# Scores ahead of their maxima, low key parts above zeros, staged keys and a full-height join in a hybrid attention and experts kernel

## The chip, the cores and the metric

The kernel runs on 1 core of one Trainium2 chip. The metric is device time in microseconds (us), as a median over executions. The engines named below are TensorE (PE, with its weight loads shown apart as PEld), VectorE (DVE), ScalarE (ACT), GpSimd (POOL) and SyncE (SP), which here only issues transfers.

## What is computed

One layer over 512 tokens of width 1024, all in float32. A normalized input is projected to many heads, three attentions follow, gates weigh them, and a routed layer of 16 experts ends it:

```python
n = rmsnorm(h, g_mix[l])
aq, ak, av, iq, ik, iw, bq, bk, bv, mq = split_cols(n @ w_in[l], IN_SPLITS)
y_a = dsa_attention(aq, ak, av, iq, ik, iw)        # top 128 of the keys by an index score, 8 heads
y_b = dilated_attention(bq, bk, bv)                # 3 groups (dilation 1, 4, 16) x 8 heads, joined by their lse
y_m = memory_attention(mq, rmsnorm(mem, g_mem[l]), w_mem_kv[l])   # 4 heads over 256 memory rows
merged = sum_i gates[i] * (y_i @ w_branch[l, i])
h = h + merged @ w_out[l]
h = h + hier_moe(rmsnorm(h, g_ffn[l]), ...)        # 16 experts, two per token
return rmsnorm(h, g_final)
```

In the dilated attention each group gives a softmax output and a log-sum-exp per head; a softmax over the three log-sum-exps joins the groups.

## The kernel before, in words

**Precision.** Every float32 operand is split into a high and a low part, and a product is three matmuls (high·high, high·low, low·high). In the attentions the two parts of a query of 64 values lie above each other: the high part in rows 0 to 63, the low part in rows 64 to 127 (`restack_q`). The keys lie the same way, but with the same part twice: `k2` holds the high part in both halves, `kl` the low part in both halves (`restack_k`, line 532). `scores` (line 255 through the helper `mm`) then takes two matmuls, queries against `k2` and queries against `kl`, with all 128 rows in each.

**Order of the work.** Up to about 505 us the projections run in one stream: for each weight block of 128x1024 a transfer is issued from POOL's queue (L113), ACT writes the high part (L139), DVE or, for blocks 14 to 45, POOL writes the low part (L143, L141), and PE multiplies (tiles `P`). Attention work is cut into segments that are fed into this stream by a count of projection steps (`feed`, `feed_att`, `tick`): `segA` makes scores and softmax, `segB` transposes the probabilities (tiles `T`, L681, L816, L890), `segC` multiplies with the values (tiles `O`). The top-k search of the first attention (`topk_seg`, L611 and L612) runs on DVE in the same way. The framework works out all waits, and puts the instructions of each engine in an order at compile time; each engine then runs its own list in that order, and an instruction that waits holds up those behind it.

**Scores and softmax.** A PSUM tile `S` (two buffers) holds the scores of two blocks of queries, u = 0 and u = 1. For each u in turn `segA` writes the scores and calls `softmax_tile`: DVE adds the mask and takes the maxima into `st` or `dl` (L628), ACT takes the exponential and the row sums (L630). The framework orders a PE write after an earlier DVE read of the same PSUM bank, so the scores of u = 1 wait for the maxima of u = 0.

**Keys and queries of a job.** The dilated attention runs in six jobs (`JOBS`: D0 twice, D12 four times), with the two jobs of the first attention between them. `rope_unit` makes rotated queries or keys in four DVE products and writes high and low parts to two tiles `st` (ACT L504, DVE L505; tag `st`, two buffers, for queries and keys alike). From there SP issues small transfers of 64 KB: 16 for the queries of a job (L522), 32 for the keys (L532). `k2` and `kl` share four buffers of tag `k2`, two tiles each.

**The join.** After the last job, `betas` makes the weights of the groups as `e2` (128 tokens x 32 columns per block), PE transposes them to 32 rows (L760), ACT copies them to `eT` of 32 rows, and `y_pair` spreads them over 128 rows by eight matmuls of 32 rows with a 0/1 matrix `pick` (tiles `T` from `eT`), whose results DVE multiplies into the outputs (L783, L784). They stand among the last gate projections, at 496 to 505 us.

**The rest.** From 505 us come the branch products (`B`), the output projection, routing, and from about 755 us the experts (`A`, `Y`).

Of the kernel before, what the change touches and what calls it, by code (L numbers as in the profile page):

```python
# [237 lines left out]
def hybrid_kernel(ctx, tc, A, out):  # L238
    nc = tc.nc
# [101 lines left out]

    def stat_x(i):
        rsx[i] = cst.tile([128, 4], F32, name="rsm", tag="rsm", bufs=3)
        scr = ap_.tile([128, 1024], F32, name="scr", tag="k2", bufs=4)
        rms(xt(i), scr, rsx[i])

    def norm_x(i):
# [130 lines left out]
    def lhs_nat(t, k):  # L478
        return nTh[:, k, 128 * t:128 * t + 128], nTl[:, k, 128 * t:128 * t + 128]

    def rope_unit(perm, then):

        t = {}

        def first():
            for i, tab in ((1, cosT), (3, sinT)):
                t[i] = rp.tile([128, 512], F32, name="t%d" % i, tag="rt", bufs=4)
                nc.vector.tensor_mul(t[i], PA, tab)

        def second():  # L490
            for i, tab in ((2, sinT), (4, cosT)):
                t[i] = rp.tile([128, 512], F32, name="t%d" % i, tag="rt", bufs=4)
                nc.vector.tensor_mul(t[i], PB, tab)
            res = []
            for (a, b, op) in ((t[1], t[2], OP.subtract), (t[3], t[4], OP.add)):
                st = rp.tile([128, 2, 512], F32R, name="st", tag="st", bufs=2)
                nc.vector.tensor_tensor(a, a, b, op=op)  # L497
                if perm:
                    av = a.rearrange("p (i r) -> p r i", r=4)
                    s0 = st[:, 0].rearrange("p (r i) -> p r i", r=4)  # L500
                    s1 = st[:, 1].rearrange("p (r i) -> p r i", r=4)
                else:
                    av, s0, s1 = a, st[:, 0], st[:, 1]
                nc.scalar.copy(s0, av)  # L504
                nc.vector.tensor_sub(s1, av, s0.bitcast(F32))  # L505
                res.append(st)
            then(res)

        PA = proj_T(None)
        feed("rope", [first], 1)  # L510
        PB = proj_T(None)
        feed("rope", [second], 1)
# [11 lines left out]
    def restack_k(sts, dsts):  # L524

        for c, d in enumerate(dsts):
            for hl in range(2):
                for half in range(2):
                    s = sts[half].bitcast(F32)
                    for dup in range(2):  # L530
                        r0 = 64 * dup + 32 * half
                        nc.sync.dma_start(d[hl][r0:r0 + 32], s[32 * c:32 * c + 32, hl])  # L532

# [23 lines left out]
        held.append(job)  # L557
        return ap_.tile([128, 2, 512], F32R, name="q2", tag="q2", bufs=4)

    def new_k2():  # L560
        return ap_.tile([128, 2, 512], F32R, name="k2", tag="k2", bufs=4)


    acc_d = dr.tile([512 + CAP, 1024], F32, name="acc_d")

    akst = ap_.tile([128, 2, 512], F32R, name="akst")
    aklo = ap_.tile([128, 2, 512], F32R, name="aklo")
    iq2 = []

    def iq_then(sts):  # L570
# [3 lines left out]

    def ik_then(sts):
        ik["k"] = new_k2()
        akf, alf, ikf = akst.bitcast(F32), aklo.bitcast(F32), ik["k"].bitcast(F32)
        restack_k(sts, [(akf[:, j], alf[:, j]) for j in range(2)] + [(ikf[:, 0], ikf[:, 1])])

# [58 lines left out]
    def dil_job(kind, j, q2, k2, kl, V):  # L638
# [7 lines left out]
        def segA(n):  # L646
            hh, head, tp = items[n]

            def f():
                S = ps.tile([128, 512], F32, name="S", tag="S", bufs=2)  # L650
                P = ap_.tile([128, 512], F32, name="Pt", tag="Pt", bufs=5)
                D[n]["P"] = P
                for u in range(2):
                    r = 2 * tp + u
                    s = slice(128 * r, 128 * r + 128)
                    c0 = 256 * u
                    if kind == "D12":
                        for g in range(2):
                            c = 2 * hh + g
                            scores(S[:, c0 + 128 * g:c0 + 128 * g + 128], q2[c // 2], c, s,  # L660
                                   k2[c // 2][:, c % 2, s], kl[c // 2][:, c % 2, s])
                        softmax_tile(S[:, c0:c0 + 256], pmask, P[:, c0:c0 + 256],
                                     st12[:, 0, r, head:head + 1], st12[:, 1, r, head:head + 1])
                    else:
                        c = hh
                        lo = 1 if r == 0 else 0
                        ks = slice(128 * (r - 1 + lo), 128 * r + 128)
                        reg = slice(c0 + 128 * lo, c0 + 256)
                        scores(S[:, reg], q2[c // 2], c, s, k2[c // 2][:, c % 2, ks], kl[c // 2][:, c % 2, ks])
                        softmax_tile(S[:, reg], gmask[:, 128 * lo:], P[:, reg],  # L670
                                     st0[:, 0, r, head:head + 1], st0[:, 1, r, head:head + 1])
            return f

        def segB(n):
# [65 lines left out]
    def betas():  # L740
# [10 lines left out]
        nc.vector.tensor_mul(e[:, 0], e[:, 0], M)  # L751
        nc.vector.tensor_mul(e[:, 1], e[:, 1], M)

        e2 = ap_.tile([128, 4, 2, 2, 8], F32R, name="e2", tag="V", bufs=2)
        et = e.rearrange("p s r h -> p r s h")
        nc.vector.tensor_copy(e2[:, :, 0], et)
        nc.vector.tensor_sub(e2[:, :, 1], et, e2[:, :, 0].bitcast(F32))
        T = ps.tile([32, 512], F32, name="T", tag="T", bufs=2)
        for t_ in range(4):
            nc.tensor.transpose(T[:, 128 * t_:128 * t_ + 128], e2[:, t_].bitcast(F32).rearrange("p a s h -> p (a s h)"),  # L760
                                ident)
        eT = ap_.tile([32, 512], F32R, name="eT", tag="Pt", bufs=5)
        nc.scalar.copy(eT, T)
        cmb["eT"] = eT

    def pick_rows():

        pick = ap_.tile([32, 16, 64], F32R, name="pick", tag="q2", bufs=4)
        nc.gpsimd.tensor_tensor(pick, ident[0:32, 0:16].unsqueeze(2).to_broadcast([32, 16, 64]),
                                ident[0:32, 16:32].unsqueeze(2).to_broadcast([32, 16, 64]), op=OP.add)  # L770
        cmb["pick"] = pick

# [85 lines left out]
    def mem_job(h, mq):  # L858
# [5 lines left out]
        def segA(tp):  # L864
            def f():
# [3 lines left out]
                for u in range(2):  # L869
# [2 lines left out]
                    mm(S[:, reg], mq[:, 0, s], kh, True, False)  # L872
                    mm(S[:, reg], mq[:, 0, s], kl_, False, False)
                    mm(S[:, reg], mq[:, 1, s], kh, False, True)
                    softmax_tile(S[:, reg], zcol.to_broadcast([128, 256]), P[:, reg], l[:, 2 + u:3 + u],
                                 l[:, u:u + 1], sc)
                r = cst.tile([128, 2], F32, name="dr_", tag="dr_", bufs=4)
# [40 lines left out]
    def mem_norm(t):  # L918
        def f():
            xm = memx[:, t]  # L920
            sm = cst.tile([128, 4], F32, name="rsm", tag="rsm", bufs=3)
            scr = ap_.tile([128, 1024], F32, name="scr", tag="k2", bufs=4)
            rms(xm, scr, sm)
            nc.vector.tensor_scalar(xm, xm, sm[:, 0:1], None, op0=OP.mult)
        return f
# [24 lines left out]
    feed_att("idx", [idx_seg(i, h) for i in range(1, 4) for h in range(4)], 10, 10)  # L950
    feed("top", [topk_seg(i, r, r + 1) for i in range(1, 4) for r in range(16)], 22, 70)
    drain("mem")
    mk = [new_k2(), new_k2()]
    mv, mqs = {}, {}

    def mem_k(h):
# [34 lines left out]
    for kind, j in JOBS:  # L991
# [14 lines left out]
        if Oall is None:  # L1006
            drain(*last)
            Oall = [yp.tile([128, 4, 512], F32, name="Oall", tag=t) for t in ("b0", "b1")]
        q2, k2, kl = [], [], []

        def q_then(sts, q2=q2, job=(kind, j)):
            q2.extend([new_q2(job), new_q2(job)])
# [2 lines left out]
        def k_then(sts, kind=kind, j=j, q2=q2, k2=k2, kl=kl, V=V, last=last):  # L1015
            drain(*last)
            k2.extend([new_k2(), new_k2()])
            kl.extend([new_k2(), new_k2()])
            restack_k(sts, [(k2[c // 2].bitcast(F32)[:, c % 2], kl[c // 2].bitcast(F32)[:, c % 2])
                            for c in range(4)])  # L1020
            feed_att((kind, j), dil_job(kind, j, q2, k2, kl, V), 7, 14)
        rope_unit(perm, q_then)
        rope_unit(perm, k_then)
        last = ((kind, j),)


# [827 lines left out]
```

## Time and profile before

| | |
|---|---|
| median of 3 runs | 1047.48 us (1044.34 to 1047.7) |
| profiled execution | 1045.13 us, its span 1043.2 us |
| PE busy | 995.0 us (95%) |
| PE weight loads busy | 788.6 us (76%) |
| DVE busy | 767.2 us (74%) |
| ACT busy | 591.9 us (57%) |
| POOL busy | 209.7 us (20%) |
| mean granted TensorE clock | 0.985 of full |

The profiled execution lies 1.93 us above its span, which is what surrounds the first and the last instruction. The ends of matmuls are modelled, so busy PE time says that work was there, not at which rate it ran; idle time of PE, and the steps between the starts of matmuls, say more. A granted clock of 1.00 is the upper level of TensorE's two (2.4 GHz), 0.50 the lower (1.2 GHz); a value between them is a mix over the stretch.

### The profile page before, as it was taken

To read this page: it belongs to the slowest core of one execution; us is meant where nothing else is said; L and a number is where in the kernel's file an instruction comes from. 1 tells how busy PE (TensorE), PEld (TensorE's weight loads), DVE (VectorE), ACT (ScalarE), POOL (GpSimd) and SP (SyncE) were. 2 spreads that over 40 slices of the span, in tenths; PEclk is the share of its full clock that TensorE was granted. 3 is DMA by queue.
4 is the path that set the end of the run, shared out by engine and by line. 5 is a ranking of instruction groups with operands and counts; after the bars stand their busy time and mean duration, and the time that the engine had idled before them with its cause. 6 is when DMAs were issued, how large, how long until landed. Compare 5 with 4: busy or idle time off the path is not lost.

```text
span 1043.2 us, 15086 instructions
## 1 busy us (share of the span) xinstructions
PE 995.0 (95%) x5102; PEld 788.6 (76%) x5102; DVE 767.2 (74%) x1433; ACT 591.9 (57%) x989; POOL 209.7 (20%) x210
## 2 busy tenths in 40 slices
PE   8998998999899999999999999998999999999994
PEld 7887887777877878787688888885677777777763
DVE  6658999957579688755743545447899999999985
ACT  6434533634366555489332334333588888888874
POOL 1124433423341000100301010023212111212102
PEclk9998999999999999999999999999999999999997
DMA  7272236463544545353543233867899999999982
GB/s 267 86 205 80 81 98 172 136 182 107 166 140 119 170 120 144 101 154 94 205 142 101 81 101 101 306 225 261 243 374 357 367 362 367 358 367 371 356 307 84
DMA packets 73414, 210.24 MB, mean 202 GB/s; under 512 B 14321, under 2 KB 14897, under 8 KB 73330
## 3 DMA queue, kind: packets, MB, share of 16 engines
q1 hardware_dynamic: 53058, 143.13, 39.3%
q0 software_dynamic: 17200, 61.88, 20.1%
q10 hardware_dynamic: 3072, 4.20, 1.1%
q8 instruction: 42, 0.69, 0.3%
q14 instruction: 42, 0.34, 0.1%
HBM read 169.11 MB, written 12.26 MB: 174 GB/s over the span
## 4 chain that ended last, share of the span: by engine, by line
PE 72%; DVE 14%; ACT 6%; DMA 3%; issue 2%; SPq 2%; ACTq 1%; POOL 0%; DVEq 0%; POOLq 0%
PE P L255 26%; PE A L255 21%; PE Y L255 11%; PE B L255 6%; PE O L255 2%; PE S L255 2%; DVE idxw L612 2%; DVE m L611 2%; SPq L532 1%; ACT Pt L630 1%; DVE st L505 1%; DMA V<-vst 1%; DVE t L497 1%; PE T L1400 1%; DVE Pt L628 1%
## 5 line engine op out<-in xcount | busy, mean ns | idle before, releaser
L255 PE MATMUL P<-nTh,whi 128*128 128x512 f32 x480 | 193.4, 403 | 0.2 <-DVE q L977 0.2
L255 PE MATMUL P<-nTh,wlo 128*128 128x512 f32 x480 | 190.5, 397 | 0.3 <-POOL wlo L141 0.3
L255 PE MATMUL P<-nTl,whi 128*128 128x512 f32 x480 | 190.2, 396 | 0.0
L139 ACT CAST whi<-wraw 128x1024 fp32r<-128x1024 f32 (+1 forms) x96 | 100.2, 1046 | 155.3 <-PE P L255 94.3
L143 DVE TENSOR_TENSOR wlo<-wraw,whi 128x1024 fp32r<-128x1024 f32 (+1 forms) x64 | 77.5, 1213 | 73.6 <-ACT whi L139 73.5
L255 PE MATMUL A<-whi,xT 128*96 128x512 f32 x384 | 126.7, 397 | 0.7 <-ACT xT L1402 0.7
L113 POOL DMA_DIRECT2D wraw<-in_w_p_dram x92 | 50.1, 545 | 359.1 <-DVE wlo L143 255.4
L255 PEld LDWEIGHTS P<-nTh,wlo 128*128 128x128 f32 x480 | 90.9, 189 | 18.6 <-POOL wlo L141 0.6
L141 POOL TENSOR_TENSOR wlo<-wraw,whi 128x1024 fp32r<-128x1024 f32 x32 | 76.4, 2388 | 141.0 <-ACT whi L139 140.9
L255 PEld LDWEIGHTS P<-nTh,whi 128*128 128x128 f32 x480 | 91.2, 190 | 16.6 <-issue 1.1
L255 PEld LDWEIGHTS P<-nTl,whi 128*128 128x128 f32 x480 | 91.2, 190 | 15.4 <-issue 0.5
L255 PEld LDWEIGHTS A<-whi,xT 128*96 128x96 f32 x384 | 61.8, 161 | 27.0 <-ACT xT L1402 0.8
L255 PE MATMUL A<-wlo,xT 128*96 128x512 f32 x192 | 75.6, 394 | 0.0
L221 DVE TENSOR_TENSOR wlo<-mraw,whi 128x1024 fp32r<-128x1024 f32 x57 | 68.7, 1222 | 3.2 <-ACT whi L220 3.0
L220 ACT CAST whi<-mraw 128x1024 fp32r<-128x1024 f32 x57 | 59.8, 1049 | 14.2 <-PE A L255 6.4
L255 PE MATMUL S<-k,q 128*128 128x128 f32 (+3 forms) x264 | 51.3, 292 | 12.5 <-DVE st L628 4.9
L255 PE MATMUL B<-yhl,whi 128*128 128x512 f32 x192 | 60.7, 396 | 1.0 <-DVE yhl L1055 1.0
L255 PEld LDWEIGHTS S<-k,q 128*128 128x128 f32 x264 | 41.7, 194 | 25.4 <-DVE st L628 10.8
L255 PE MATMUL Y<-whi,hT 128*96 128x512 f32 x180 | 59.9, 399 | 0.0
L635 DVE TENSOR_TENSOR PT<-T,PT 128x512 fp32r<-128x512 f32 (+1 forms) x60 | 39.6, 668 | 25.1 <-ACT PT L634 24.4
L255 PE MATMUL P<-whi,nTh 128*128 128x256 f32 (+1 forms) x176 | 51.8, 294 | 0.1
L255 PE MATMUL P<-whi,nTl 128*128 128x256 f32 (+1 forms) x176 | 51.5, 293 | 0.0
(367 smaller groups left out, 2241.5 us busy)
## 6 DMA issues: line engine op xcount, KB each, us to landing
wraw<-in_w_p_dram POOLq DMA_DIRECT2D x92, 512.0 KB, 4.0
mraw<-in_w_exp_dram SPq DMA_DIRECT2D x77, 512.0 KB, 8.1
yraw<-in_w_exp_dram SPq DMA_DIRECT2D x52, 512.0 KB, 8.1
hraw<-in_w_exp_dram SPq DMA_DIRECT2D x48, 512.0 KB, 8.1
k<-st SPq DMA_DIRECT2D x200, 64.0 KB, 2.2
q<-st SPq DMA_DIRECT2D x144, 64.0 KB, 2.3
wraw<-in_w_exp_dram SPq DMA_DIRECT2D x10, 512.0 KB, 8.1
V<-vst ACTq DMA_DIRECT2D x64, 64.0 KB, 2.1
```

The costliest lines, as they stand in the source:

```text
L113: (self.nc.sync if i < NAV + 2 else self.dma).dma_start(t[:, :n], ap)
L139: self.nc.scalar.copy(hi[:, :n], raw[:, :n])
L141: self.nc.gpsimd.tensor_tensor(lo[:, :n], raw[:, :n], hi[:, :n].bitcast(F32), op=OP.subtract)
L143: self.nc.vector.tensor_sub(lo[:, :n], raw[:, :n], hi[:, :n].bitcast(F32))
L220: self.nc.scalar.copy(hi, raw)
L221: self.lo_ins.append(self.nc.vector.tensor_sub(lo, raw, hi.bitcast(F32)))
L255: return nc.tensor.matmul(o, lhsT=l, rhs=r, start=start, stop=stop)
L497: nc.vector.tensor_tensor(a, a, b, op=op)
L505: nc.vector.tensor_sub(s1, av, s0.bitcast(F32))
L611: nc.vector.max(m8, acc)
L612: nc.vector.match_replace(out=acc, in_to_replace=m8, in_values=acc, imm_value=-3.0e38)
L635: nc.vector.tensor_sub(hl[:, 1, :n], T[:, :n], hl[:, 0, :n].bitcast(F32))
```

## The change

Four edits.

1. In `segA` of the dilated and of the memory attention the scores of both query blocks of a tile `S` are written first, and the two calls of `softmax_tile` follow. (The first attention, `dsa_job`, keeps one tile `S` per head and is not touched.)
2. The low part of the keys is written into rows 0 to 63 only; rows 64 to 127 of its tiles are zero. A job's keys take 24 transfers where they took 32. The low tiles of all dilated jobs are two fixed tiles `kz`, set to zero once on POOL; `k2` has two buffers. The memory attention's keys use the buffers of `kz` earlier. `aklo` and the low half of the index keys get a POOL fill with zeros too.
3. The keys of every dilated job but the first are written to a tile `stk` in the place of the first job's values `V0` (tag `yb`), in place of the two `st` buffers; the segments of the job before are all put into the stream ahead of it.
4. `e2` has 128 columns (32 used, the rest zero), so that its transposes, `eT` and `pick` have 128 rows, those above 32 zero; POOL sets `e2` and `pick` to zero.

```diff
-    def rope_unit(perm, then):
+    def rope_unit(perm, then, stage=None):
...
-            for (a, b, op) in ((t[1], t[2], OP.subtract), (t[3], t[4], OP.add)):
-                st = rp.tile([128, 2, 512], F32R, name="st", tag="st", bufs=2)
+            own = None if stage is None else stage()
+            for n, (a, b, op) in enumerate(((t[1], t[2], OP.subtract), (t[3], t[4], OP.add))):
+                st = rp.tile([128, 2, 512], F32R, name="st", tag="st", bufs=2) if own is None else own[:, n]
...
-                    for dup in range(2):
+                    for dup in range(2 - hl):
                         r0 = 64 * dup + 32 * half
                         nc.sync.dma_start(d[hl][r0:r0 + 32], s[32 * c:32 * c + 32, hl])
...
-    def new_k2():
-        return ap_.tile([128, 2, 512], F32R, name="k2", tag="k2", bufs=4)
+    def new_k2(tag="k2"):
+        return ap_.tile([128, 2, 512], F32R, name=tag, tag=tag, bufs=2)
+
+    def zero_below(t):
+        nc.gpsimd.memset(t[64:128].bitcast(F32), 0.0)
...
     aklo = ap_.tile([128, 2, 512], F32R, name="aklo")
+    zero_below(aklo)
...
         ik["k"] = new_k2()
+        zero_below(ik["k"][:, 1])
...
+                later = []
                 for u in range(2):
...
-                        softmax_tile(S[:, c0:c0 + 256], pmask, P[:, c0:c0 + 256],
-                                     st12[:, 0, r, head:head + 1], st12[:, 1, r, head:head + 1])
+                        later.append((S[:, c0:c0 + 256], pmask, P[:, c0:c0 + 256],
+                                      st12[:, 0, r, head:head + 1], st12[:, 1, r, head:head + 1]))
...
+                for a in later:
+                    softmax_tile(*a)
...
-        e2 = ap_.tile([128, 4, 2, 2, 8], F32R, name="e2", tag="V", bufs=2)
+        e2 = cmb["e2"]
+        ev = e2[:, :, 0:32].rearrange("p r (a s h) -> p r a s h", a=2, s=2)
...
-        T = ps.tile([32, 512], F32, name="T", tag="T", bufs=2)
+        T = ps.tile([128, 512], F32, name="T", tag="T", bufs=2)
...
-        eT = ap_.tile([32, 512], F32R, name="eT", tag="Pt", bufs=5)
+        eT = ap_.tile([128, 512], F32R, name="eT", tag="Pt", bufs=5)
...
-        pick = ap_.tile([32, 16, 64], F32R, name="pick", tag="q2", bufs=4)
-        nc.gpsimd.tensor_tensor(pick, ident[0:32, 0:16].unsqueeze(2).to_broadcast([32, 16, 64]),
+        cmb["e2"] = ap_.tile([128, 4, 128], F32R, name="e2", tag="V", bufs=2)
+        nc.gpsimd.memset(cmb["e2"].bitcast(F32), 0.0)
+        pick = ap_.tile([128, 16, 64], F32R, name="pick", tag="q2", bufs=4)
+        nc.gpsimd.memset(pick.bitcast(F32), 0.0)
+        nc.gpsimd.tensor_tensor(pick[0:32], ident[0:32, 0:16].unsqueeze(2).to_broadcast([32, 16, 64]),
...
-    mk = [new_k2(), new_k2()]
+    mk = [new_k2("kz"), new_k2("kz")]
...
+            kz = [new_k2("kz"), new_k2("kz")]
+            for z in kz:
+                zero_below(z)
-        q2, k2, kl = [], [], []
+        q2, k2, kl = [], [], kz
...
-            kl.extend([new_k2(), new_k2()])
...
+        def stage_k(last=last):
+
+            drain(*last)
+            return yp.tile([128, 2, 2, 512], F32R, name="stk", tag="yb")
         rope_unit(perm, q_then)
-        rope_unit(perm, k_then)
+        rope_unit(perm, k_then, None if (kind, j) == JOBS[0] else stage_k)
```

The memory attention's `segA` (in `mem_job`) is cut in two loops over u in the same way, and the scratch tiles of tag `k2` have two buffers instead of four.

## Rows read from the trace of the kernel before

**Rows 1.** Windows by stage: from:to, length, busy us per engine, clock, DMA share.
```profile
56.00:140.00 84.00, 76.79 (x471) 67.44 (x470) 65.72 (x174) 40.94 (x85) 29.02 (x23) 0.96 0.35 110
140.00:205.00 65.00, 61.14 (x351) 51.39 (x350) 61.62 (x149) 30.14 (x66) 26.37 (x18) 1.00 0.54 154
205.00:300.00 95.00, 86.61 (x510) 74.67 (x508) 58.54 (x115) 38.62 (x80) 34.76 (x24) 0.96 0.52 151
...
440.00:505.00 65.00, 64.26 (x308) 48.64 (x306) 38.83 (x91) 48.60 (x87) 9.48 (x12) 1.00 0.41 121
...
760.00:1010.00 250.00, 250.00 (x1191) 177.53 (x1190) 230.82 (x234) 214.16 (x256) 42.86 (x40) 1.00 1.02 361
```

The engines of these rows are PE, PEld, DVE, ACT and POOL, in this order, with their instructions behind; the last figure is GB/s.

**Rows 2.** Waits of PE's matmuls: us in total, times, longest.
```profile
PE S L255 <- DVE st L628: 4.9, 6, 1.8
PE T L681 <- ACT Pt L630: 4.3, 7, 1.6
PE S L255 <- DMA k<-st: 3.9, 4, 1.8
PE S L255 <- DVE dl L628: 3.5, 1, 3.5
```

**Rows 3.** Waits of PE's weight loads, same columns.
```profile
PEld S L255 <- DVE st L628: 10.8, 17, 2.2
...
PEld S L255 <- DVE dl L628: 6.0, 7, 3.9
```

**Rows 4.** Timeline of a memory tile: start, us, engine, form, [idle before <-releaser].
```profile
92.51 0.51 PE L255 MATMUL S<-k,q 128*128 128x256 f32 x3
...
96.75 0.42 DVE L628 CUSTOM_DVE_ANT_0 Pt<-S,zcol 128x256 f32<-128x256 f32 x1
...
97.22 1.01 PE L255 MATMUL S<-k,q 128*128 128x256 f32 x3 [3.52 <-DVE dl L628]
97.26 0.51 ACT L630 ACTIVATE Pt<-Pt,dl 128x256 f32<-128x256 f32 x1 [4.95 <-DVE dl L628]
...
101.41 1.69 DVE L881 TENSOR_SCALAR Pt<-Pt,dr__1029 128x256 f32<-128x256 f32 x2
...
103.35 0.27 PE L890 MATMUL T<-ident,Pt 128*128 128x128 f32 x1
```

**Rows 5.** Timeline of SP's queue and of ACT around one job's keys.
```profile
260.46 23.23 SPq L532 DMA_DIRECT2D k<-st  x32
...
285.39 0.62 ACT L504 CAST st<-t 128x512 fp32r<-128x512 f32 x1 [0.38 <-DMA k<-st]
```

**Rows 6.** Timeline of the join, PE and DVE.
```profile
500.65 0.50 PE L255 MATMUL T<-eT,pick 32*128 32x512 f32 x1
...
501.08 0.50 PE L255 MATMUL P<-nTh,whi 128*128 128x512 f32 x1
...
501.18 1.11 DVE L784 TENSOR_TENSOR Oall<-Oall,T 128x512 f32<-128x512 f32 x1 [0.28 <-PE T L255]
...
501.74 0.50 PE L255 MATMUL T<-eT,pick 32*128 32x512 f32 x1
...
502.27 0.69 DVE L783 TENSOR_TENSOR yb<-Oall,T 128x512 f32<-128x512 f32 x1
```

**Rows 7.** Chain that ended last, a stretch of gates: start, us, what, count.
```profile
529.36 10.92 PE P L255 x48
```

**Rows 8.** Groups of POOL: busy us, mean ns, idle before and releaser.
```profile
L141 POOL TENSOR_TENSOR wlo<-wraw,whi 128x1024 fp32r<-128x1024 f32 x32 | 76.4, 2388 | 141.0 <-ACT whi L139 140.9
...
L1842 POOL MEMSET const-float32-0.0<- 128x1 f32 x1 | 0.1, 98 | 0.2 <-issue 0.2
```

**Rows 9.** Timeline of POOL and DVE, one product beside POOL's work and one alone.
```profile
236.98 2.37 POOL L141 TENSOR_TENSOR wlo<-wraw,whi 128x1024 fp32r<-128x1024 f32 x1 [0.86 <-ACT whi L139]
237.23 2.67 DVE L497 TENSOR_TENSOR t<-t,t 128x512 f32<-128x512 f32 x1
...
242.51 0.68 DVE L497 TENSOR_TENSOR t<-t,t 128x512 f32<-128x512 f32 x1
```

More of the change, by code (lines that the diff above doesn't have):

```diff
@@ L343, in stat_x @@
         rsx[i] = cst.tile([128, 4], F32, name="rsm", tag="rsm", bufs=3)
-        scr = ap_.tile([128, 1024], F32, name="scr", tag="k2", bufs=4)
+        scr = ap_.tile([128, 1024], F32, name="scr", tag="k2", bufs=2)
         rms(xt(i), scr, rsx[i])
@@ L669, in f @@
                         scores(S[:, reg], q2[c // 2], c, s, k2[c // 2][:, c % 2, ks], kl[c // 2][:, c % 2, ks])
-                        softmax_tile(S[:, reg], gmask[:, 128 * lo:], P[:, reg],
-                                     st0[:, 0, r, head:head + 1], st0[:, 1, r, head:head + 1])
+                        later.append((S[:, reg], gmask[:, 128 * lo:], P[:, reg],
+                                      st0[:, 0, r, head:head + 1], st0[:, 1, r, head:head + 1]))
+                for a in later:
+                    softmax_tile(*a)
             return f
@@ L752, in betas @@
         nc.vector.tensor_mul(e[:, 1], e[:, 1], M)
-        e2 = ap_.tile([128, 4, 2, 2, 8], F32R, name="e2", tag="V", bufs=2)
+        e2 = cmb["e2"]
+        ev = e2[:, :, 0:32].rearrange("p r (a s h) -> p r a s h", a=2, s=2)
         et = e.rearrange("p s r h -> p r s h")
-        nc.vector.tensor_copy(e2[:, :, 0], et)
-        nc.vector.tensor_sub(e2[:, :, 1], et, e2[:, :, 0].bitcast(F32))
-        T = ps.tile([32, 512], F32, name="T", tag="T", bufs=2)
+        nc.vector.tensor_copy(ev[:, :, 0], et)
+        nc.vector.tensor_sub(ev[:, :, 1], et, ev[:, :, 0].bitcast(F32))
+        T = ps.tile([128, 512], F32, name="T", tag="T", bufs=2)
         for t_ in range(4):
-            nc.tensor.transpose(T[:, 128 * t_:128 * t_ + 128], e2[:, t_].bitcast(F32).rearrange("p a s h -> p (a s h)"),
-                                ident)
-        eT = ap_.tile([32, 512], F32R, name="eT", tag="Pt", bufs=5)
+            nc.tensor.transpose(T[:, 128 * t_:128 * t_ + 128], e2[:, t_].bitcast(F32), ident)
+        eT = ap_.tile([128, 512], F32R, name="eT", tag="Pt", bufs=5)
         nc.scalar.copy(eT, T)
@@ L874, in f @@
                     mm(S[:, reg], mq[:, 1, s], kh, False, True)
+                for u in range(2):
+                    reg = slice(256 * u, 256 * u + 256)
                     softmax_tile(S[:, reg], zcol.to_broadcast([128, 256]), P[:, reg], l[:, 2 + u:3 + u],
@@ L921, in f @@
             sm = cst.tile([128, 4], F32, name="rsm", tag="rsm", bufs=3)
-            scr = ap_.tile([128, 1024], F32, name="scr", tag="k2", bufs=4)
+            scr = ap_.tile([128, 1024], F32, name="scr", tag="k2", bufs=2)
             rms(xm, scr, sm)
```

## The prediction

> **What bounds the kernel now.** I read the windows by stage first, to see where PE has time to give. Over 760 to 1010 us PE is busy for all of 250 us [rows 1]: nothing the change touches lies there, and a gain made earlier only moves that stage forward. The transfers are as full there (share 1.02), but they start when the stages before free their buffers, so they move along. From 56 to 205 us, from 205 to 300 and from 440 to 505 PE is idle for 7.2 + 3.9, 8.4 and 0.7 us (length less busy time) [rows 1]. In two of these stages the mean clock is 0.96; 0.04 of 84 us and of 95 us are 3.4 and 3.8 us of full-speed work lost to the lower level. So the change plays for some 20 us of idle time and 7 us of clock, no more.
>
> Next I read the waits, to see what ended PE's idle time. Matmuls into `S` waited 4.9 us for maxima of the dilated attention, 3.5 us in one piece for a maximum of the memory attention, and 3.9 us for keys on their way; transposes waited 4.3 us for exponentials [rows 2]. The weight loads of the same score matmuls show 10.8 and 6.0 us for the maxima [rows 3]. The true loss lies between the two, since the modelled end of a matmul covers part of a wait, while a weight load that waits does not always delay a matmul.
>
> Last I read the timeline of the longest wait. The scores of u = 0 go out at 92.51 us; DVE, behind in its list, takes their maxima only at 96.75, and PE stands until 97.22 with the scores of u = 1 [rows 4]. The same three matmuls that took 0.51 us before the wait take 1.01 behind it [rows 4]: the clock has fallen to its lower level, 1.2 GHz, after those 3.52 us of idle time.
>
> **The change part by part.** The sum is made against the profiled execution, 1045.13 us, which lies 2.35 us below the median of 1047.48.
>
> *Scores ahead of maxima.* Both u's scores are ready at once and no longer wait for DVE. What this can give at most is 4.9 + 3.5 = 8.4 us by the matmuls and 16.8 us by the weight loads [rows 2, 3]; at least it gives nothing, because DVE's own work is unchanged and what is late next is the transpose, which needs the exponentials. I work out the memory tile. DVE would take both maxima from 96.75 on, to 97.6 (two of 0.42). Two exponentials of 0.51 us and the two divisions, 1.69 together [rows 4], bring the probabilities to about 100.3. PE would be at the transpose sooner than that: it would wait there instead, and go on at 100.3, not 103.35. That is 3.0 us, part of it from the clock. But up to 205 us DVE is nearly full, 61.62 of 65 us from 140 on [rows 1], and only 3.4 us of slack can take up a PE that runs earlier. I keep 2.0 of the 3.0. Of the 4.9 us for `st` I keep 2.0 too: some of these waits lie in the stage where DVE is full, others are waits for one of the two `S` buffers, which stay. Together 4.0 us, bounds 0 and 16.8.
>
> *Low parts above zeros.* A job's 32 key transfers take SP 23.23 us, 0.73 us each [rows 5]. A set of keys for one head takes 8 of them, and 6 after the change: the first of the four sets is complete 1.5 us earlier, the last 5.8. PE waited four times for keys, 3.9 us in all, at longest 1.8 [rows 2]; an advance of 1.5 to 5.8 us covers nearly all. I take 3.3 us, bounds 0 (if something else is late there) and 3.9. The matmuls are as many and as long as before. The queries' transfers that follow on SP go out 5.8 us earlier, which only helps.
>
> *Zeros from POOL.* Six fills: `aklo`, the low index keys, two `kz`, `e2`, `pick`. No fill of this size is in the trace. One lies between 0.1 us (128x1) and 2.39 us (a 128x1024 difference of two operands) [rows 8]; as a fill reads nothing, I take about 1 us, an estimate between the two. POOL is busy 29 of 84 us in the first stage and 9.5 of 65 in the last [rows 1], and that idle time hides them. The cover could fail for the two `kz`, which wait for the last memory scores with weight splits queued behind them on POOL, in a stretch in which DVE has no slack: the bound is 2 x 2.39 = 4.8 us. POOL's work can also slow DVE: a product of two tiles took 2.67 us beside POOL's difference and 0.68 alone [rows 9]. I take a cost of 0.3 us. The Trainium skill ("SBUF — State Buffer", Who interferes with whom) says that a DVE instruction with two SBUF inputs contends with a GpSimd instruction that reads SBUF, not with one that only writes it. By that rule a fill would leave those products alone and the bound on this side would be near 0, by the row 4.8 us; no fill of such a size in this trace decides it.
>
> *Staged keys.* The `st` buffers then serve queries alone. ACT waited 0.38 us for the transfers of keys out of `st` [rows 5]; that goes, worth at most 0.4, and I take 0.3. In exchange the second job's staging waits until the first job's last value product has read `V0`. By the count of projection steps the first job's segments end 21 steps after they are fed, the next job's key staging comes after 24; so the earlier drain moves nothing, here or in later jobs, whose segments also end before.
>
> *The join at full height.* A matmul `T` of 32 rows comes every 1.09 us (500.65 to 501.74) with two projections between, of which one stands in [rows 6]; three matmuls at the ordinary step, 10.92 / 48 = 0.23 us [rows 7], would take 0.68. So 0.41 us go on each passage from 128 rows to 32 and back, 3.3 us for eight. DVE limits what comes of it: a pair of `T` takes it 1.11 + 0.69 = 1.80 us [rows 6], against 2.18 for a pair now, so 0.38 x 4 = 1.5 us is the most. I take 1.0, bounds 0 and 1.5. The zeros' fill and the wider copy lie ahead of it: ACT's copy has as many columns as before.
>
> *Sum.* 4.0 + 3.3 + 1.0 + 0.3 - 0.3 = 8.3 us. From the profiled execution this gives 1036.8, from the median 1039.2; I forecast 1038 us.
>
> **The rivals.** *The waits come back at the transposes.* DVE is what PE is behind, so scores that go out earlier only make the transposes wait longer. For it: DVE at 61.62 of 65 us [rows 1], and 4.3 us of waits for exponentials already [rows 2]. Against it: from 205 to 300 us DVE has 36 us of slack. The gain is then that of the keys, half eaten up, and of the join: 1.7 + 1.0 + 0.3 = 3.0, so 1044.5 us from the median.
>
> *The clock stays up.* If the two stretches at the lower level also vanish, 3.4 + 3.8 = 7.2 us are added, to 15.5 in all: about 1031 us. For it: the first follows the very wait that is removed [rows 4]. Against it: by the working above PE then stands at the transpose nearly as long.
>
> *The waits come in fewer, longer pieces.* A PE that runs ahead through all the scores it may, and then stands once at a transpose, can fall to the lower clock where short waits did not make it fall. A fall costs some 3.4 to 3.8 us, as in the two stages with clock 0.96 [rows 1]. Without the scores' 4.0 us the gain is 4.3; from the third new fall on the kernel is slower by over 0.3%: 4.3 - 3 x 3.6 = -6.5, about 1054 us. The place is 100 to 205 us, where DVE is late most often. Against it: of all the waits in rows 2 only one is over 2 us.
>
> **How the numbers follow.** Changes within 0.3% (3.1 us) are about what a measurement of this kernel can't tell from none; that is 1044.3 to 1050.6 us. The forecast holds 0.47, with its own range of 1033 to 1043. Waits come back: 0.27, of which 0.10 ends below 1044.3 and 0.17 within. Clock stays up: 0.11. Longer pieces: 0.15, of which 0.13 slower and 0.02 within. So faster 0.68, the same 0.19, slower 0.13. The range of 1029 to 1047 holds the forecast, the first rival, and most of the second; it leaves out the third and the lower end of the second.
>
> **What would show it.** Right: no scores wait for maxima inside a tile, so the rows of waits for `st` and `dl` fall from 8.4 us to under 3; the keys' wait falls below 1 us and a job's keys take SP 17 us (24 x 0.73); in the join the step around `T` falls to about 0.23 us, with DVE's pairs back to back; the idle time of PE from 56 to 300 us falls from 19.5 to about 13. Wrong: waits of transposes for exponentials that grow from 4.3 us by as much as the scores' waits fell; a clock below 0.96 in either stage; a wait of PE for the low parts made on POOL near 140 us; or ACT held at the staged keys of the second job. The order of instructions on each engine is set anew, and small shifts of it that no row foretells could move the sum by a few us either way.

## The result, and the profile after

| | before | after |
|---|---|---|
| median | 1044.02 us (1043.29 to 1047.70, 6 runs) | 1039.45 us (1034.89 to 1041.09, 6 runs) |
| profiled execution (span) | 1045.13 us (1043.2) | 1038.59 us (1036.8) |
| mean granted clock | 0.985 | 0.981 |

The ratio is 0.9935 with a 95% interval of 0.9916 to 0.9954: faster by some 6.8 us (4.8 to 8.8). This ratio is not that of the two medians (0.9956, or 4.6 us). The total came near the sum of 8.3 us; its parts did not come as forecast. First the waits of PE's matmuls, in us, times, longest:

```profile
PE T L907 <- DVE Pt L898: 6.3, 3, 4.6
PE S L255 <- DMA k<-stk: 4.0, 2, 3.8
PE T L831 <- DVE Pt L824: 2.5, 4, 1.1
...
PE S L255 <- DMA kz<-stk: 2.1, 1, 2.1
PE T L693 <- ACT Pt L638: 1.7, 5, 1.0
...
PE S L255 <- DMA k<-st: 1.0, 1, 1.0
```

Against [rows 2]: no score waits for a maximum any more, where it was 8.4 us. But the waits for keys went from 3.9 to 4.0 + 2.1 + 1.0 = 7.1 us, and the transposes of the memory tiles (L907) now wait 6.3 us for its divisions. Next the windows of the stages in [rows 1], with the same columns:

```profile
56.00:140.00 84.00, 77.43 (x481) 68.60 (x480) 71.57 (x187) 40.52 (x85) 32.63 (x25) 0.98 0.35 105
140.00:205.00 65.00, 62.47 (x367) 53.27 (x366) 62.39 (x144) 30.02 (x67) 27.24 (x20) 1.00 0.51 146
205.00:300.00 95.00, 85.59 (x500) 75.12 (x499) 53.13 (x116) 40.24 (x84) 32.82 (x23) 0.95 0.50 145
...
440.00:505.00 65.00, 62.50 (x304) 48.48 (x303) 40.15 (x92) 50.28 (x90) 11.96 (x14) 1.00 0.48 145
...
760.00:1010.00 250.00, 249.43 (x1186) 176.87 (x1185) 229.73 (x232) 212.62 (x254) 41.11 (x39) 1.00 1.03 361
```

From 56 to 205 us PE is idle for 9.1 us (11.1 before), from 205 to 300 for 9.4 (8.4 before), with the clock at 0.95 (0.96 before). The stage where the keys were to come in time is no better than it was. Two places show why. The memory tile of [rows 4], in PE's and DVE's timeline:

```profile
90.44 0.87 PE L255 MATMUL S<-kz,q 128*128 128x256 f32 x6
92.53 0.87 PE L255 MATMUL S<-kz,q 128*128 128x256 f32 x6
...
96.92 0.41 DVE L636 CUSTOM_DVE_ANT_0 Pt<-S,zcol 128x256 f32<-128x256 f32 x1
...
97.25 0.42 DVE L636 CUSTOM_DVE_ANT_0 Pt<-S,zcol 128x256 f32<-128x256 f32 x1
...
99.02 0.61 DVE L898 TENSOR_SCALAR Pt<-Pt,dr__1025 128x256 f32<-128x256 f32 x2
...
99.42 1.06 PE L907 MATMUL T<-ident,Pt 128*128 128x128 f32 x4 [4.59 <-DVE Pt L898]
```

Both blocks' scores are out at 93.4 us without a wait, both maxima are taken back to back, and PE stands at the transpose: the wait of 3.52 us has become one of 4.59 at the next thing that DVE delivers. The transpose goes at 99.42 (forecast: 100.3). The shorter pair of divisions accounts for the 0.9 us between the two: it takes 0.61 us here, where the pair of 1.69 in [rows 4], from which the forecast was worked out, had a weight split of POOL beside it. In POOL's timeline of the kernel before:

```profile
100.31 2.37 POOL L141 TENSOR_TENSOR wlo<-wraw,whi 128x1024 fp32r<-128x1024 f32 x1 [8.17 <-ACT whi L139]
```

The second place is the third job's keys, that of [rows 5], in DVE's, ACT's, SP's and PE's timelines:

```profile
248.93 0.69 DVE L495 TENSOR_TENSOR t<-P,sinT 128x512 f32<-128x512 f32 x1 [2.18 <-PE P L255]
...
250.13 3.29 DVE L500 TENSOR_TENSOR t<-t,t 128x512 f32<-128x512 f32 x2
252.86 2.15 ACT L507 CAST stk<-t 128x512 fp32r<-128x512 f32 x2 [3.06 <-DVE t L500]
253.99 2.41 SPq L535 DMA_DIRECT2D k<-stk  x4
...
268.71 1.16 SPq L535 DMA_DIRECT2D kz<-stk  x2
...
264.97 0.44 PE L255 MATMUL S<-k,q 128*128 128x128 f32 x1 [3.79 <-DMA k<-stk]
```

SP issues the job in 15.9 us (253.99 to 269.87) where it took 23.23. Yet the time from the first issue to the score that waits is 264.97 - 253.99 = 11.0 us; before, it was 271.84 - 260.46 = 11.4. The clock of the two stretches behind this wait (same columns as the windows above):

```profile
260.00:270.00 10.00, 6.21 (x34) 6.04 (x33) 6.33 (x10) 2.22 (x5) 2.90 (x2) 0.68 0.76 200
270.00:280.00 10.00, 10.00 (x72) 10.00 (x72) 3.64 (x12) 3.69 (x13) 0.00 (x0) 0.80 0.29 86
```

0.32 and 0.20 of ten microseconds each are 5.2 us of full-speed work lost around one wait of 3.79 us. In the kernel before, the same place had a wait of 1.84 us and a clock of 1.00; it loses its 3.8 us of this stage [rows 1] elsewhere, so that over the whole stage (0.05 of 95 us, 4.8) the change loses only 1 us more.

The waits say little of when work is done; the place in the stream of projections says more. This table (worked out from the starts of the `P` matmuls in the traces, one profiled execution each) shows by how many us a kernel is ahead of the kernel before at its k-th projection matmul; the experiments' columns are used below.

```
k-th P   before us | after   e1    e3    e5    e6    e7    e9    e10   e11
300        76.01   |  1.9   1.0   0.7   3.9   0.9   0.4   0.8   0.3   0.4
780       205.79   |  3.4   0.1   1.6   0.9   0.6   0.5   1.9   1.0   2.5
960       254.92   |  6.4   1.4   2.3   5.4   5.1   3.2   4.3   0.1   6.0
1080      281.18   |  1.5   2.2   2.4   2.9   9.0   0.0   1.5   3.9  10.3
1260      338.62   |  2.9  -0.6   1.8   3.7   3.6   1.4   2.9  -7.3   4.2
1620      439.51   |  6.6  -0.7   1.8   5.1   8.3   5.1   6.6  -6.0   6.5
1800      494.79   |  6.5   0.0   1.7   5.0   9.3   5.0   6.6  -5.1   7.5
first B   505.18   |  8.2   0.0   3.4   6.6   7.8   6.6   6.6  -7.6   5.3
```

After is ahead by 6.4 us at 255 us, loses 4.9 at the keys, wins them back by 440 us, and gains 1.6 in the join. How far to trust it: e7, which below turns out to have the same order of instructions on every engine as after, differs from it by up to 3.2 us at one position, and e3, with the order of the kernel before ahead of the join, is 1.7 us ahead there. So a difference under some 3 us at one position can't be told from one execution to the next. In the columns with a delay of 10 (e6, e10, e11) attention work stands later among the projections, so that up to 340 us being ahead is in part work put off.

### The profile page after: what moved, and what is told of

Read it like the earlier page. It is cut to its first block, busy times and chain, and to the rows that moved or that the text cites. A ratio compares the mean times of both kernels' runs of the same rounds, so it can differ in the third digit from the quotient of the medians.

```text
span 1036.8 us, 14992 instructions
## 1 busy us (share of the span) xinstructions
PE 991.2 (96%) x5102; PEld 793.0 (76%) x5102; DVE 764.0 (74%) x1433; ACT 590.0 (57%) x989; POOL 214.6 (21%) x216
## 4 chain that ended last, share of the span: by engine, by line
PE 64%; DVE 6%; ACT 5%; SPq 2%; issue 1%; DMA 1%; ACTq 0%; POOL 0%; POOLq 0%; DVEq 0%
PE A L255 21%; PE P L255 19%; PE Y L255 11%; PE B L255 6%; SPq L535 2%; PE S L255 2%; PE O L255 1%; ACT Pt L638 1%; PE T L1424 1%; DMA kz<-stk 1%; ACT whi L139 1%; ACT PT L642 1%; PE T L693 1%; PE T L831 1%; PE T L1497 1%
## 5 line engine op out<-in xcount | busy, mean ns | idle before, releaser
L255 PEld LDWEIGHTS P<-nTl,whi 128*128 128x128 f32 x480 | 90.4, 188 | 15.5
L255 PE MATMUL P<-wlo,nTh 128*128 128x256 f32 (+1 forms) x176 | 53.0, 301 | 0.0
L221 DVE TENSOR_TENSOR wlo<-yraw,whi 128x1024 fp32r<-128x1024 f32 x39 | 46.8, 1220 | 2.5 <-ACT whi L220 2.4
```

The lines of the kernel that those rows point to most:

```text
L221: self.lo_ins.append(self.nc.vector.tensor_sub(lo, raw, hi.bitcast(F32)))
L255: return nc.tensor.matmul(o, lhsT=l, rhs=r, start=start, stop=stop)
```

## The experiments

Each ratio is against the kernel before on the same chip. That kernel's median was between 1044.02 and 1047.95 us from one chip to the next, so kernels of different groups are compared by their ratios, with an interval whose half width is the root of the summed squares of theirs.

**One edit at a time.** e1 has edit 1 alone, e2 edit 2, e3 the join (edit 4), e4 the staged keys (edit 3).

```diff
e1: + later.append((S[:, c0:c0 + 256], pmask, P[:, c0:c0 + 256], ...
    + for a in later:
    +     softmax_tile(*a)
e2: - for dup in range(2):
    + for dup in range(2 - hl):
e3: - eT = ap_.tile([32, 512], F32R, name="eT", tag="Pt", bufs=5)
    + eT = ap_.tile([128, 512], F32R, name="eT", tag="Pt", bufs=5)
e4: - rope_unit(perm, k_then)
    + rope_unit(perm, k_then, None if (kind, j) == JOBS[0] else stage_k)
```

> Only edit 1 (scores of both query blocks ahead of their maxima); all else as before. Theory 1 (the scores carry the change: the 8.4 us of waits for maxima go, and most of that is kept where DVE and the keys have slack): 3 to 6 us faster, ratio 0.994 to 0.997, no wait of S for st or dl inside a tile, a longer wait for keys near 265 us than in the changed kernel's 3.8 us, since the keys' transfers are still 32. Theory 2 (the keys and the join carry it, the scores' gain is given back at the transposes): within 1.5 us of before.

> Only edit 2 (low key parts above zeros, 24 transfers for a job's keys). Theory 1: the keys' chain of products, copies and transfers is late by less than PE's other waits, so 0 to 1.5 us faster. Theory 2 and the prediction's own term: the 3.9 us of waits for keys nearly vanish, 3.3 us faster.

> Only edit 4 (the join over 128 rows). Both theories: 0.5 to 1.5 us faster, with the gain between 490 and 505 us and none ahead of it; the step around a T matmul falls from 1.09 to near 0.7 us with DVE as the limit. A rival: nothing, since the branch products wait for DVE's work on y anyway.

> Only edit 3 (later jobs' keys staged in the first values' place). Both theories: 0 to 0.5 us, not to be told from before. A rival: slower by 1 us or more, if the second job's staging waits for the last reader of the first job's values.

| edit alone | median us | before us | ratio |
|---|---|---|---|
| e1 scores | 1046.21 | 1047.04 | 0.9995 [0.9985, 1.0005] |
| e2 zeros | 1044.87 | 1047.04 | 0.9983 [0.9965, 1.0000] |
| e3 join | 1042.18 | 1047.04 | 0.9957 [0.9944, 0.9971] |
| e4 staging | 1044.22 | 1047.04 | 0.9979 [0.9964, 0.9994] |

The edit that the sum gave the most is worth nothing alone. The waits of e1:

```profile
PE S L255 <- DMA k<-st: 6.3, 4, 2.4
PE T L896 <- DVE Pt L887: 5.0, 3, 2.7
```

The waits for `st` and `dl` are gone and have come back at the keys (3.9 to 6.3 us) and the memory tiles' transposes (1.8 to 5.0). e2's waits for keys are 5.4 + 1.8 us, no less than before. The join alone gave far more than the 1.0 us of the sum: of the 4.9 us that its profiled execution is faster than before's, 1.7 lie ahead of the join, where the order of instructions is the same, 1.6 in it (1.7 to 3.4 in the table), and the rest behind it. In this pair of executions both of the other parts can be the clock: from 56 to 140 us it is 0.98 in e3 and 0.96 before, from 662 to 760 us 1.00 and 0.98, and 0.02 of 84 and of 98 us are 1.7 and 2.0 us of full-speed work.

**The whole less one edit.** e5 is the changed kernel without edit 1, e9 without the join, e12 without the staged keys; e8 keeps all but makes 32 key transfers a job again, without the fills for them.

```diff
e8: - for dup in range(2 - hl):
    + for dup in range(2):
    - nc.gpsimd.memset(t[64:128].bitcast(F32), 0.0)
```

> The changed kernel with edit 1 undone (each block's maxima right behind its scores, as before); edits 2, 3 and 4 stay. Theory 1 (the scores carry the change): 1 to 3 us faster than before, ratio 0.997 to 0.999. Theory 2 (keys and join carry it): 4 to 7 us faster, ratio 0.993 to 0.996.

> The changed kernel with the low key parts written to both halves again (32 transfers a job, no fill below); all else as changed, the fixed low tiles too. If the transfers' number sets the time at which the keys are there, the waits at 230 and 265 us grow by 1.5 us or more each and the kernel is 2 to 5 us slower than the changed one, ratio to before 0.996 to 0.999. If the products, the copies and the landing set it: within 1 us of the changed kernel.

> The changed kernel with the old join of 32 rows (edits 1 to 3). Theory A: the join is worth what its own stretch shows, about 1.6 us from the steps of its matmuls and DVE pairs, so the whole without it stays at 0.995 of the time before (0.9935 + 0.0015), within 0.994 to 0.9965. Rival B: the join alone measured 0.9957, and it is worth that within the whole as well (4.5 us): 0.9978, within 0.9965 to 0.999. The trace should show the eight matmuls of 32 rows again at about 1.09 us a step in either case.

> The changed kernel without the staged keys (edits 1, 2 and 4; the keys go through the two buffers st again). Theory A: staging frees only the 0.4 us that ACT waited for transfers out of st, so the whole without it is 0.9935 to 0.995. Rival B: with staging the keys' last products no longer wait behind the queries' transfers, and it is worth what it measured alone (0.9979, 2.2 us) or more: 0.9955 to 0.998, with ACT or DVE seen waiting for transfers out of st and waits of PE for keys above the 7.1 us of the changed kernel.

| the whole without | median us | before us | ratio |
|---|---|---|---|
| e5 scores | 1043.11 | 1046.17 | 0.9979 [0.9960, 0.9998] |
| e8 the 24 transfers | 1039.67 | 1046.17 | 0.9940 [0.9916, 0.9964] |
| e9 the join | 1037.51 | 1047.95 | 0.9902 [0.9877, 0.9926] |
| e12 the staging | 1039.53 | 1047.95 | 0.9914 [0.9891, 0.9937] |
| (nothing: the change) | 1039.45 | 1044.02 | 0.9935 [0.9916, 0.9954] |

Only edit 1 is clearly missed: without it the kernel is slower than the change by 4.6 us (1.8 to 7.4). For the other three no loss is seen, but the intervals are wide: taking out the 24 transfers costs 0.5 us (-2.7 to 3.7), the join -3.4 (-6.7 to -0.2), the staging -2.2 (-5.3 to 0.9). All ranges expected for e9 lay above what was measured; for e12 staging was expected to be worth nothing (0.9935 to 0.995) or 2.2 us and more, and the first is nearer. The gains measured alone (the four sum to 0.86%) and the losses of leaving out thus do not match edit by edit, and for the join and the staging the two sides disagree. For the join, a matmul step can be read. Of e9, with 32 rows, and of the change, PE's timeline:

```profile
494.07 0.50 PE L255 MATMUL T<-eT,pick 32*128 32x512 f32 x1
495.16 0.50 PE L255 MATMUL T<-eT,pick 32*128 32x512 f32 x1
496.25 0.49 PE L255 MATMUL T<-eT,pick 32*128 32x512 f32 x1
```

```profile
494.17 0.40 PE L255 MATMUL T<-eT,pick 128*128 128x512 f32 x1
495.05 0.51 PE L255 MATMUL T<-eT,pick 128*128 128x512 f32 x1
495.86 0.39 PE L255 MATMUL T<-eT,pick 128*128 128x512 f32 x1
```

The step is 1.09 us in the one and some 0.85 in the other, where DVE's pairs set it. The matmuls of e9 come in the same order as those of the change, and at the 1800th projection the two are level (6.6 and 6.5). What e9 loses then (1.6 us at the first `B` in the table) it has back, and more, in the routing, which no edit touches. That window of e9 and of the change:

```profile
662.00:760.00 98.00, 92.52 (x477) 68.93 (x476) 69.69 (x193) 45.08 (x77) 22.50 (x24) 1.00 0.82 284
```

```profile
662.00:760.00 98.00, 92.65 (x463) 69.07 (x462) 66.98 (x191) 43.23 (x74) 22.74 (x24) 0.97 0.79 269
```

The clock is 1.00 in the one and 0.97 in the other, and 0.03 of 98 us are 2.9 us. That is one execution of each; whether the clock of that stage hangs on the kernel, the runs don't settle.

**Who makes PE wait at the keys.** e6 feeds the segments of a dilated job 10 projection steps after its keys, not 7. e7 moves the top-k search 10 steps back instead, to see whether it is what makes DVE late at the memory tile.

```diff
e6: - feed_att((kind, j), dil_job(kind, j, q2, k2, kl, V), 7, 14)
    + feed_att((kind, j), dil_job(kind, j, q2, k2, kl, V), 10, 14)
e7: - feed("top", [topk_seg(i, r, r + 1) for i in range(1, 4) for r in range(16)], 22, 70)
    + feed("top", [topk_seg(i, r, r + 1) for i in range(1, 4) for r in range(16)], 32, 60)
```

> The changed kernel with the dilated jobs' segments fed 10 projection steps after the keys are issued, where it is 7. Theory A (the scores' gain is eaten at 230 and 265 us, where PE now arrives before the keys, 16 us from the last key product to the score): the waits of 2.1 and 3.8 us and the low clock behind them go, 4 to 8 us faster than the changed kernel, ratio to before 0.986 to 0.990. Rival B (PE only runs into DVE or ACT a little further on, at the transposes): within 2 us of the changed kernel.

> The changed kernel with the top-k search started 10 steps later (32 for 22, over 60 steps for 70, so that it ends at the same step). Theory A (at 94 to 99 us PE waits 4.6 us at the first transpose of the memory attention because DVE has top-k and index work ahead of the maxima in its list): that wait shrinks by 1 to 3 us, 1 to 3 us faster than the changed kernel. Rival B: DVE is full until 205 us whatever the order, so what is gained at 99 us is lost before 205, within 1 us of the changed kernel.

e6: 1036.52 against 1046.17 us, 0.9897 [0.9869, 0.9925], the lowest median here, though not told apart from e9's; against the change it gains 4.0 us (0.4 to 7.5), at the lower end of the 4 to 8 that theory A expected. The wait of 3.79 us is gone, and with it the fall of the clock at that place (windows of e6):

```profile
260.00:265.00 5.00, 5.00 (x38) 4.73 (x37) 3.30 (x3) 1.05 (x1) 2.91 (x2) 1.00 0.71 196
265.00:270.00 5.00, 4.76 (x41) 4.65 (x40) 3.52 (x9) 1.59 (x3) 0.62 (x2) 1.00 0.75 219
```

Over the whole profiled execution the mean clock is 0.984 all the same (0.981 in the change): it falls at other places.

e7: 1039.08 against 1046.17 us, 0.9933 [0.9913, 0.9954], as the change. It answers nothing about the top-k search, because the edit did not reach the chip: in the two traces every engine has the same instructions in the same order, and eight steps of the search (L619, L620) stand ahead of the first memory maximum in both. So e7 is the change measured once more. What holds DVE at the memory tile can be read from its timeline (e7's; the last line is PE's):

```profile
98.12 0.73 DVE L608 SCALAR_TENSOR_TENSOR idxw<-R,iw,idxw 128x512 f32<-128x512 f32 x1
...
99.36 0.42 DVE L619 MAX8 m<-idxw 128x8 f32<-128x256 f32 x1
99.70 0.41 DVE L636 CUSTOM_DVE_ANT_0 Pt<-S,zcol 128x256 f32<-128x256 f32 x1
...
102.20 1.11 PE L907 MATMUL T<-ident,Pt 128*128 128x128 f32 x4 [4.58 <-DVE Pt L898]
```

From 95.0 to 99.7 us DVE is busy for 4.63 of 4.70 us, with top-k and index work (L606 to L620) up to the maximum. What a list without them there would give was not measured.

**Edit 1 with and without a PE that is early at the keys.** e10 is the kernel before, e11 is e1, both with the delay of 10 steps.

> The kernel before, with one number changed: the dilated segments are fed 10 projection steps after the keys of their job instead of 7. Theory A (the chain of products, casts, issue and landing takes about 16 us, which 7 steps do not cover): the 3.9 us of waits for keys vanish and the kernel gains 2 to 4 us, 0.996 to 0.998. Rival B: the same wait is simply met at the next thing that is late (maxima or exponentials), 0.999 to 1.001.

> Edit 1 alone (scores ahead of the maxima) together with the delay of 10 steps. Edit 1 alone measured 0.9995 with waits for keys of 6.3 us. Theory A: its gain was eaten by the keys, which come no earlier for a PE that runs ahead; with the keys out of the way it is worth 3 to 4 us over the kernel before with the delay of 10 alone, so 0.992 to 0.995. Rival B: its gain comes back as waits of transposes, whatever the keys do; then it equals the kernel before with the delay of 10 within 1 us.

| | scores as before | scores ahead of maxima |
|---|---|---|
| delay 7 | 1 | e1 0.9995 [0.9985, 1.0005] |
| delay 10 | e10 1.0057 [1.0036, 1.0078] | e11 0.9930 [0.9906, 0.9955] |

Neither theory foresaw e10: the delay alone makes the kernel 6 us slower. And e11, which differs from it in edit 1 only, is 1.2% faster. Of e10, waits of PE, the longest of them in PE's timeline, and two windows:

```profile
PE S L255 <- DVE st L628: 8.2, 7, 3.3
PE S L255 <- DVE dl L628: 4.5, 2, 3.5
...
240.15 0.89 PE L255 MATMUL S<-k,q 128*128 128x128 f32 x6 [3.31 <-DVE st L628]
...
240.00:250.00 10.00, 9.62 (x37) 7.62 (x38) 4.92 (x14) 3.99 (x11) 2.00 (x1) 0.66 0.45 122
290.00:300.00 10.00, 9.19 (x36) 7.14 (x35) 5.21 (x14) 3.81 (x9) 3.17 (x3) 0.69 0.69 191
```

The same two windows of e11:

```profile
240.00:250.00 10.00, 8.52 (x46) 7.00 (x47) 7.31 (x21) 5.89 (x14) 2.96 (x2) 1.00 0.51 142
290.00:300.00 10.00, 8.55 (x45) 6.52 (x44) 8.69 (x20) 4.28 (x9) 4.80 (x4) 1.00 0.44 141
```

In DVE's timeline of e10, with the scores in the old order, the maximum that PE waits for stands behind two products of the rotation and a low part (in the kernel before behind one product, [rows 9]):

```profile
234.63 3.49 DVE L497 TENSOR_TENSOR t<-t,t 128x512 f32<-128x512 f32 x2
238.69 1.06 DVE L505 TENSOR_TENSOR st<-t,st 128x512 fp32r<-128x512 f32 x1 [0.57 <-ACT st L504]
239.68 0.40 DVE L628 CUSTOM_DVE_ANT_0 Pt<-S,masks 128x256 f32<-128x256 f32 x1
```

The wait for it is 3.31 us (1.8 at most before), and the clock falls to 0.66 and, 50 us later, to 0.69, which is 3.4 + 3.1 = 6.5 us of full-speed work. The kernel before loses 3.8 us in this stage too [rows 1], so against it some 3 us are new there. With edit 1 PE passes that place, and the clock stays at 1.00 from 205 to 300 us. The clock tells the kernels apart beyond the one execution that was profiled: its mean is 0.978 to 0.981 in all seven executions of e10, 0.982 to 0.989 in the twelve of the kernel before beside it, 0.986 to 0.989 in the six of e11. Theory A of e11 stands in its direction (edit 1 is worth more when the keys are not next), but its size, 3 to 4 us, was too small by far: 1054.18 - 1041.51 = 12.7 us. How much of that is the clock and how much idle time was not separated. And a part of theory A in e10 fell: the waits for keys were 4.3 us with the delay of 10, not gone.

## Why the prediction was right, and where it was not

**Scores ahead of maxima (4.0 us, bounds 0 to 16.8).** The mechanism is shown: the waits for `st` and `dl` fell from 8.4 us to none, and PE waits at the transpose of the memory tile as foreseen, which goes at 99.42 and not the worked 100.3 because of the shorter divisions. By the ratios, the edit is worth 0.9979 - 0.9935 = 0.0044, some 4.6 us (1.8 to 7.4), in the company of the others; the two profiled executions differ by only 1.1 us (1039.71 and 1038.59). The figure fits, but it is not the edit's own: alone 0.5 us (interval -0.5 to 1.6), beside later-fed segments 12.7. The step that the prediction lacked is that the wait moves along PE's list to what is late next, not to the transposes alone: in e1 it came back at the keys.

**Low parts above zeros (3.3 us).** The mechanism of this step failed: the waits for keys rose from 3.9 to 7.1 us, where they were to fall below 1. "An advance of 1.5 to 5.8 us covers nearly all" took SP's issue for what sets the end. SP did fall to 15.9 us a job, near the 17 foretold, but the time from the first issue to the score that waits (the third of the job) did not follow. Times from the first issue, in us:

```
          transfers   P matmuls ahead   a weight block   the score   wait there
                      of the score      lands            starts      us
before    32          1031              10.7             11.4        1.84
e3        32          1031              10.6             11.3        1.72
e4        32          1031               9.1              9.9        0.31
e8        32          1031              10.0             10.6        1.09
e2        24          1022              10.7             11.0        3.41
after     24          1018              10.7             11.0        3.79
e9        24          1018              10.9             11.4        4.19
e12       24          1022              10.3             10.7        3.09
```

(Worked out from the starts and landings in the traces.) Issue and landing of what the score needs take 9.9 to 11.4 us with 32 transfers and 10.7 to 11.4 with 24. The traces tell what the score waits behind: in each of these kernels POOL issues a weight block's transfer of 512 KB 4.7 or 4.8 us after the first key, and the score starts 0.3 to 0.9 us after that block has landed. In before and after, the key issued just ahead of the block lands 2.0 us after its issue, the one issued just behind it 5.6 and 5.3 us. With 32 transfers all four keys of the third score are issued behind the block; with 24 two of them still are. In e4 the block lands 1.6 us sooner than in e3, and the score starts 1.4 us sooner. No run moved the block, so this is read from the traces and not tried.

What edit 2 does change is the order: in the six kernels with it that score stands behind 1018 or 1022 projection matmuls in PE's list, in the five without it (delay 7) behind 1031, in e1 1032. Thirteen matmuls at 0.23 us [rows 7] are 3.0 us by which PE comes earlier, to keys that land nearly when they did. The order is made at compile time; that it counts on the shorter issue was not tried, but with 32 transfers, in e8, it is 1031 again. What the edit is worth stays open: alone 1.8 us (0.0 to 3.7), in the whole 0.5 (-2.7 to 3.7), so that even 3.3 us of time are not excluded. e8 waits less for keys than the change (4.9 us) and more for exponentials (5.5 us, against 1.7).

**Zeros from POOL (-0.3).** The three largest took what was estimated at 1 us, in POOL's groups:

```profile
L567 POOL MEMSET kz<- 64x1024 f32 x2 | 2.0, 1012 | 3.5 <-PE S L255 3.4
...
L783 POOL MEMSET pick<- 128x1024 f32 x1 | 1.0, 975 | 0.0
```

All six are 5.0 us, and PE's list of waits has none for `wlo` (0.3 us before). But fills do slow DVE. In DVE's and POOL's timeline:

```profile
110.71 0.95 POOL L567 MEMSET kz<- 64x1024 f32 x1 [3.41 <-PE S L255]
...
110.87 1.20 DVE L898 TENSOR_SCALAR Pt<-Pt,dr__1156 128x256 f32<-128x256 f32 x2
...
127.46 1.08 POOL L567 MEMSET kz<- 64x1024 f32 x1
...
127.31 1.38 DVE L898 TENSOR_SCALAR Pt<-Pt,dr__1327 128x256 f32<-128x256 f32 x2
```

The pair of divisions that took 0.61 us alone (99.02 above) takes 1.20 and 1.38 beside a fill: 0.6 and 0.8 us more, on the engine that PE waits for in that stage. These instructions have one SBUF tensor as input. The Trainium skill ("SBUF — State Buffer", Who interferes with whom) says that a DVE instruction with two SBUF inputs does not contend with a GpSimd instruction that only writes, and counts `tensor_scalar` among those that can take the port pair shared with GpSimd; the two pairs agree with the second. The prediction weighed the rule for another kind of instruction than the one that met the fills. No run shows what the fills cost in time; the cost of 0.3 us stays an assumption.

**Staged keys (0.3).** e4 measured 2.2 us alone (interval 0.6 to 3.8), beyond the 0.4 that ACT waited; in the whole e12 shows no worth (-2.2 us, -5.3 to 0.9). ACT's wait of 0.38 us in [rows 5] does not reach the lower end of what e4 gained alone; what made e4 faster stays open.

**The join (1.0, bounds 0 to 1.5).** The mechanism held and the size was a little low: 1.6 us, in e3 and in after, between the 1800th projection and the first `B`. DVE's pair came every 1.70 us (493.21 to 494.90, 496.60), not 1.80, and (2.18 - 1.70) x 4 = 1.9.

**The rivals.** The first, waits that come back at the transposes, is half there: all transposes' waits in the list went from 4.3 + 2.0 + 1.8 = 8.1 us to 6.3 + 2.5 + 1.7 = 10.5, and the waits for keys grew by 3.2 us: together 5.6 of the 8.4 us came back. The second, a clock that stays up, came by half in the first stage (0.98 for 0.96) and not in the other (0.95 for 0.96); its sum, 1047.48 - 15.5, is 1032 and not 1031. The third, fewer and longer waits with a fall of the clock, is what happens at 265 us (5.2 us). In e10 a longer wait and falls of the clock come too, and 1054.18 us beside that rival's 1054 is chance: the rival had three new falls at 100 to 205 us in the changed kernel, where e10 has the old order of scores, and its falls stand at 240 and 290. Of the signs named, the idle time of PE from 56 to 300 us came to 18.5 us, not 13.

The forecast's sum came out in part by luck: the keys' 3.3 us, whose mechanism did not come, are made up by terms that were sized low. By the estimates 4.6 for the scores and 1.6 for the join are 6.2 of the 6.8 us measured, but the interval of the first alone spans 5.6 us, so this split is an account and not shown. A good part of the scores' gain comes late: between 339 and 440 us the change gains 3.7 us (2.9 to 6.6 in the table; e7 and e9, with the same order of matmuls, 3.7 each), e5, without edit 1, only 1.4.

## What to carry to other kernels

A wait that is taken from a full pipeline goes to what is late next, so price an edit by the chain that then decides, and test it both alone and left out of the whole: here one edit was worth 0.5, 4.6 and 12.7 us in three surroundings. Before transfers are made fewer, measure from their first issue to the use, and look for what lands just before the use: here a weight block from another queue. Where that time doesn't move, more distance for the consumer can help (e6: one number, 4.0 us, 0.4 to 7.5, below the change), but not in every kernel (e10: 6 us above the kernel before). An edit to one engine's work can move the compile-time order of another, as here a score 13 matmuls up, and that may cost what the edit saves. And an edit of the source can leave that order as it was (e7): compare the order of instructions before reading a result.

## What the runs showed of the hardware that was not expected

- One wait of PE can cost more in clock than in idle time: 3.31 us were followed by 3.4 us of full-speed work lost (e10 at 240 us), 3.79 us by 5.2 (the change at 265 us). The length of the wait does not set the loss: at the same place, from 260 to 290 us, 4.19 us in e9 and 3.41 in e2 left a clock of 0.94 (1.8 us lost), 3.94 us in e7, which has the change's order of instructions, one of 0.89 (3.3 us), and 3.79 in the change one of 0.83 (5.1 us). The second fall of e10 came at 290 us behind single waits of at most 1.55 us, 2.7 us of idle time in the ten microseconds before (window 280 to 290: PE busy 7.34, clock 0.96).
- A fill of 64x1024 float32 on POOL takes 0.95 to 1.08 us and doubles a pair of DVE divisions beside it (0.61 to 1.20 and 1.38 us).
- A transfer of 64 KB issued 0.4 us ahead of a 512 KB transfer on another queue landed 2.0 us after its issue, one issued 0.2 to 0.3 us behind it after 5.6 us (the kernel before) and 5.3 us (the change).
